# Latent attention's opening in another order, and the softmax sums spread over partitions by transposition and DMA instead of TensorE

## The chip, the cores and the metric

The kernel runs on one core of one Trainium2 chip. The metric is the device time of one execution in microseconds (us). Engines: TensorE (PE; its weight loads PEld), VectorE (DVE), ScalarE (ACT), GpSimd (POOL), and SyncE (SP), which here only issues DMAs.

## What is computed

Two layers of a streaming encoder on a sequence of 512 tokens, width 1024. A layer is half a SwiGLU, a mixer, half a SwiGLU, each behind an RMS norm. The first layer's mixer is pooling beside "forgetting" attention (8 heads); the second layer's is latent attention (MLA, 16 heads). The part that the change touches:

```python
def mla_mixer(h, cos, sin, w_in, q_norm, kv_norm, w_q_b, w_kv_b, w_out):
    proj = h @ w_in
    c_q  = proj[..., :256]; c_kv = proj[..., 256:384]
    k_rope = apply_rope(proj[..., 384:], cos, sin)
    q  = (rms_norm(c_q, q_norm) @ w_q_b).reshape(b, s, 16, 96)    # 64 plain + 32 rotary
    kv = (rms_norm(c_kv, kv_norm) @ w_kv_b).reshape(b, s, 16, 128) # 64 keys + 64 values
    ...
    y = blocked_attention(qk, k, v, 96 ** -0.5, CHUNK)   # softmax(q k^T + mask) v
    return y.reshape(b, s, 1024) @ w_out
```

## The kernel before

Activations lie transposed: 128 channels on the partitions, 512 tokens along the free axis. Every product is made in three passes: each operand is split into a rounded part and its rest (`hi` on ACT, `lo` on DVE, or on POOL where code says `nc.gpsimd`), and `mm3` (L178 to L180) adds rounded by rounded, rest by rounded and rounded by rest. Weights come through a ring of three raw tiles, whose loads (L189) SP issues in program order; a load waits until the split of an older tile has freed its buffer. A scheduler orders the instructions of every engine; `keep_in_program_order` holds the order of TensorE's products in the opening of MLA (`self.ordered`).

**The opening of MLA** (L1145 to L1320). `latent(n)` makes one of four projections of 24 products: 0 is the key/value latent, 1 and 2 the query latent, 3 the rotary keys. Each is multiplied by `rstdB`, the RMS factor of the incoming norm (`scaled`, L1145). `sums` (L364 to L386) sums squares by products with a column of ones (L371) and makes the factor `rt`, tokens on partitions; `spread` (L392) broadcasts `rt` over the partitions by products with the identity matrix, and ACT copies the result out of PSUM (L396). Three such factors are made: of the incoming norm, of the key/value latent (`rkv`) and of the query latent. `rotations` makes the tables `rota` and `rotb` from the last one (L1183, L1186), and a `query` is a product of 6 passes times such a table (L1248). The rotary keys are made last (L1173 to L1176).

**The heads.** Per head: scores on TensorE (mask added by L785), row minimum on DVE (L806), exponential on ACT with the row sums written into `sm` (L809), transposition of the probabilities on TensorE (L842), product with the values (`weighted`, L862, L866, L867). Two heads make a pair. After the pair's second `weighted`, `divided` takes the reciprocal of the eight columns of `sm` (L819), broadcasts it by eight products with the identity (L823, 16 records in the trace) into a bank of PSUM, and multiplies `y` by that bank (L827). `y` is then split into `yh` and `yl` for the output projection. `divided` runs for 4 pairs of the first mixer and 8 pairs of MLA. `keys_values` and `query` of the next pairs are made between the heads, and stand ready to fill TensorE while a softmax is under way.

Of the kernel before, what the change touches and what calls it, by code (L numbers as in the profile page):

```python
# [97 lines left out]
class Trunk:  # L98
    def __init__(self, ctx, tc, d, out):
        self.tc, self.nc, self.d, self.out = tc, tc.nc, d, out  # L100
        self.n = 0
        self.last = []
        self.pending = self.ordered = False
        self.then = None
        self.sums_of = []
# [257 lines left out]

    def sums(self, n, then=None):  # L364

# [11 lines left out]
        act = nc.scalar.activation  # L377
        act(root, ps[:, 0:blocks], AF.Sqrt, bias=self.eps[:, 1:2], scale=4.0 / n)
        act(ms, ps[:, 0:blocks], AF.Identity, bias=self.eps[:, 0:1], scale=1.0 / n)
        squared = act(rr, root, AF.Square, scale=0.5)  # L380
        if then is not None:
            self.table(then, squared)

# [4 lines left out]
        def spread(rstdB):  # L388

            pb = self.bank("pc")[:, 0 : blocks * P]  # L390
            for t in range(blocks):
# [3 lines left out]
                ))  # L395
            nc.scalar.activation(rstdB, pb, AF.Copy)  # L396
            self.rt = rt
# [392 lines left out]

    def probabilities(self, pool, sc, e):

# [14 lines left out]
        for i in (3, 2, 0, 1):  # L807
            bank, ps, cs = sc[i]
            self.exp = nc.scalar.activation(  # L809
                pr[bank][:, cs], ps[:, cs], AF.Exp, bias=mn[:, i : i + 1],  # L810
                scale=-1.0, accum_out=sm[:, i : i + 1],
            )
        return pr
# [127 lines left out]
    def pool_fox(self, next_col):  # L941
        nc, d = self.nc, self.d
        with self.tc.tile_pool(name=self.name("fox"), bufs=1) as pool:
# [63 lines left out]
            def head_scores(head, q1, q2, k1, k2):  # L1007
# [8 lines left out]

                return self.probabilities(pool, self.scores(block, self.causal), head % 2)

# [109 lines left out]
    def mla(self, next_col):  # L1128
        nc, d = self.nc, self.d
        wm = d["w_mla"]  # L1130
        with self.tc.tile_pool(name=self.name("mla"), bufs=1) as pool:
# [10 lines left out]

            def scaled(ps, first=None):
                t = self.temp()
                nc.vector.tensor_tensor(t, ps, self.rstdB, op=ALU.mult)  # L1145
                if first is not None:
                    self.square_into(t, first, not first)
                return t

            def parts(n, t, gcol):  # L1150
# [6 lines left out]
            rows_of = (slice(0, 64), slice(64, P))  # L1157

            self.ordered, self.pending = True, False
            rkv = ptile("rkv", dt=F32)  # L1160
            ps = latent(0)
            spread = self.sums(D)
            ps, ps1 = latent(1, 3, lambda: spread(self.rstdB)), ps
            ckv = scaled(ps1, True)
            spread_kv = self.sums(P)
            ps, ps1 = latent(2, 3, lambda: spread_kv(rkv)), ps
            cq = [parts(0, scaled(ps1, True), C_QN)]
            nc.vector.tensor_tensor(ckv, ckv, rkv, op=ALU.mult)
            ckvh, ckvl = parts(2, ckv, C_KVN)
            cq.append(parts(1, scaled(ps, False), C_QN + 1))  # L1170
            spread_q = []
            t = scaled(latent(3, 5, lambda: spread_q.append(self.sums(2 * P, AF.Exp))))
# [3 lines left out]
            nc.vector.tensor_tensor(t[0:64, :], t[0:64, :], s[0:64, :], op=ALU.add)  # L1176
            rot = [ptile("rota", dt=F32), ptile("rotb", dt=F32)]

            def rotations():
                rq = ptile("rkv", dt=F32)  # L1180
                spread_q[0](rq)
                for e in range(2):
                    nc.vector.tensor_scalar(  # L1183
                        rot[e][rows_of[e], :], rq[rows_of[e], :], -MLA_SCALE, None, op0=ALU.mult
                    )
# [3 lines left out]
                    )  # L1189


            keys = [[(self.xh[2 * e + m], self.xl[2 * e + m]) for m in range(2)] for e in range(2)]
            queries = [(self.xh[4 + m], self.xl[4 + m]) for m in range(4)]
            for e in range(2):
                for kh, _ in keys[e]:
                    self.hi(kh[rows_of[1 - e], :], t[0:64, :])
            for e in range(2):
                for _, kl in keys[e]:
                    self.lo(kl[rows_of[1 - e], :], t[0:64, :], keys[1][0][0][0:64, :])

            units = {}
            self.first = []

            def keys_values(pair):

                both = pair % 2 == 0
                cols = slice(0, 7 * P) if both else slice(7 * P, 12 * P)
                if True:
                    units[pair] = wh, wl = self.unit(
                        d["w_qkv"][pair // 2][:, cols], 5 + 2 * both, pool=pair > 0  # L1210
                    )
                m = pair % 2
                pk = self.bank("pa")
                self.mm3(pk, wh[:, 4, :], wl[:, 4, :], ckvh, ckvl, True, True)
# [14 lines left out]
                for half in range(2):  # L1229
                    pv = self.bank("pa")  # L1230
                    for t in range(2):
                        tok = slice((2 * half + t) * P, (2 * half + t + 1) * P)
                        self.mm3(pv[:, 2 * t * P : 2 * (t + 1) * P], ckvh[:, tok], ckvl[:, tok],
                                 vwh, vwl, True, True)
# [18 lines left out]
            def head_scores(head):  # L1253
# [9 lines left out]
                mask = self.chunked.rearrange("p a b -> p (a b)")  # L1263
                return self.probabilities(pool, self.scores(block, mask), head % 2)

# [15 lines left out]

            keys_values(0)
            query(0)
            query(1)
            self.ordered = False
            done = None
# [5 lines left out]
            for head in range(MLA_HEADS):  # L1292
                pr = head_scores(head)
                if head % 2 == 0 and head + 2 < MLA_HEADS:
                    keys_values(head // 2 + 1)
                if head + 2 < MLA_HEADS:
                    query(head + 2)
# [150 lines left out]
```

## Time and profile before

| | before |
|---|---|
| median of 3 runs | 1787.09 us (1785.72 to 1788.37) |
| the profiled execution | 1785.65 us |
| its span, first to last instruction | 1783.9 us |
| PE busy in the span | 1758.2 us (99%) |
| DVE, ACT, POOL busy | 1441.4, 925.2, 199.6 us |

The profile comes from one execution; its span is the time between its first and last instruction. A busy PE means that a matmul was under way. Idle time before an instruction is put down to what released it. The first mixer lies at about 395 to 525 us, MLA's opening at 1224 to 1270 us, MLA's heads up to about 1407 us.

### The profile page before, as it was taken

Reading aid. Unit: us, or ns where it says so; the run is one execution under the profiler, and the core shown is the slowest. Engines: PE = TensorE matmul, PEld = TensorE weight load, DVE = VectorE, ACT = ScalarE, POOL = GpSimd, SP = SyncE. Lnnn points to the kernel's source line nnn. Section 1 sums busy time; section 2 is a strip of 40 time slices with the busy share of each in tenths; the row PEclk is TensorE's granted clock in tenths of the full one; section 3 lists DMA queues with packets and bytes.
Section 4 is the critical chain, followed back from the end, with each engine's and each line's share of the span. In section 5 each row is a group of like instructions: output and inputs, shape, how many; then the busy total and the mean of one; then the engine's idle time right before and its main releaser. Section 6 shows DMA issues by size and latency. Waiting matters only on the chain.

```text
span 1783.9 us, 28548 instructions
## 1 busy us (share of the span) xinstructions
PE 1758.2 (99%) x11444; PEld 1586.0 (89%) x11444; DVE 1441.4 (81%) x2197; ACT 925.2 (52%) x1524; POOL 199.6 (11%) x156
## 2 busy tenths in 40 slices
PE   8999999999999999999999999999899999999998
PEld 6999999888888999999899999998788799999997
DVE  7988888657859988887699998975777799888874
ACT  7444444446647444444555444444777574444444
POOL 2000000113340000000200000002545200000002
PEclk9999999999999999999999999999999999999999
DMA  5333333313122333333233333341102123433331
GB/s 180 94 119 107 95 107 107 94 52 97 60 70 77 114 118 103 104 102 119 78 94 108 109 109 100 97 131 47 46 27 59 52 92 103 122 96 107 105 97 48
DMA packets 48933, 167.07 MB, mean 94 GB/s; under 512 B 5536, under 2 KB 7584, under 8 KB 48800
## 3 DMA queue, kind: packets, MB, share of 16 engines
q1 hardware_dynamic: 48800, 165.25, 30.3%
q8 instruction: 89, 1.46, 0.3%
q14 instruction: 44, 0.36, 0.1%
HBM read 163.14 MB, written 2.10 MB: 93 GB/s over the span
## 4 chain that ended last, share of the span: by engine, by line
PE 73%; DVE 2%; ACT 1%; issue 0%; POOL 0%; DVEq 0%; ACTq 0%; POOLq 0%
PE pa L178 10%; PE pa L180 10%; PE pa L179 10%; PE px L178 7%; PE px L180 7%; PE px L179 7%; PE pz L180 4%; PE pz L178 4%; PE pz L179 4%; PE py L180 2%; PE py L178 2%; PE py L179 2%; PE px L842 1%; PE pc L178 1%; PE pc L180 1%; PE pc L179 1%
## 5 line engine op out<-in xcount | busy, mean ns | idle before, releaser
L160 ACT ACTIVATE wh<-raw 128x1024 fp32r<-128x1024 f32 (+2 forms) x233 | 236.3, 1018 | 166.9 <-PE px L179 56.0
L165 DVE TENSOR_TENSOR wl<-raw,wh 128x1024 fp32r<-128x1024 f32 (+1 forms) x200 | 240.5, 1205 | 28.9 <-ACT wh L160 28.5
L347 POOL TENSOR_TENSOR acc<-acc,sq 128x512 f32<-128x512 f32 (+1 forms) x48 | 63.3, 1320 | 1066.1 <-ACT sq L341 1065.5
L618 DVE SCALAR_TENSOR_TENSOR h<-pa,h 128x512 f32<-128x512 f32 (+1 forms) x200 | 133.0, 666 | 58.9 <-PE pa L180 57.6
L180 PE MATMUL pa<-hh,wl 128*128 128x512 f32 (+1 forms) x432 | 165.9, 384 | 0.0
L179 PE MATMUL pa<-hl,wh 128*128 128x512 f32 (+1 forms) x432 | 165.6, 383 | 0.0
L178 PE MATMUL pa<-hh,wh 128*128 128x512 f32 (+1 forms) x432 | 165.2, 383 | 0.0
L180 PE MATMUL px<-xh,wl 128*128 128x256 f32 (+1 forms) x484 | 140.4, 291 | 0.5 <-DVE wl L165 0.5
L178 PE MATMUL px<-xh,wh 128*128 128x256 f32 (+1 forms) x484 | 139.7, 291 | 1.1 <-ACT wh L160 1.1
L179 PE MATMUL px<-xl,wh 128*128 128x256 f32 (+1 forms) x484 | 140.3, 290 | 0.0
L160 ACT ACTIVATE wh<-s 128x1024 fp32r<-128x1024 f32 (+1 forms) x51 | 51.2, 1008 | 153.0 <-PE px L179 134.3
L160 ACT ACTIVATE vh<-raw 128x1024 fp32r<-128x1024 f32 x83 | 87.7, 1059 | 72.9 <-PE px L179 38.7
L179 PE MATMUL pa<-hl,vh 128*128 128x512 f32 (+1 forms) x304 | 115.2, 380 | 0.0
L178 PE MATMUL pa<-hh,vh 128*128 128x512 f32 (+1 forms) x304 | 114.9, 381 | 0.0
L180 PE MATMUL pa<-hh,vl 128*128 128x512 f32 (+1 forms) x304 | 114.0, 380 | 0.0
L165 DVE TENSOR_TENSOR vl<-raw,vh 128x1024 fp32r<-128x1024 f32 x83 | 101.1, 1219 | 9.3 <-ACT vh L160 9.1
L178 PE MATMUL pz<-eh,wh 128*128 128x256 f32 x388 | 108.5, 280 | 0.0
L180 PE MATMUL pz<-eh,wl 128*128 128x256 f32 x388 | 108.4, 279 | 0.0
L179 PE MATMUL pz<-el,wh 128*128 128x256 f32 x388 | 108.4, 279 | 0.0
L178 PEld LDWEIGHTS px<-xh,wh 128*128 128x128 f32 x484 | 90.4, 188 | 5.8 <-ACT wh L160 1.5
L180 PEld LDWEIGHTS px<-xh,wl 128*128 128x128 f32 x484 | 90.8, 188 | 3.7 <-DVE wl L165 1.0
L179 PEld LDWEIGHTS pa<-hl,wh 128*128 128x128 f32 x432 | 81.2, 188 | 14.5
(410 smaller groups left out, 5599.0 us busy)
## 6 DMA issues: line engine op xcount, KB each, us to landing
raw<-in_w_gu_dram SPq DMA_DIRECT2D x172, 512.0 KB, 3.6
raw<-in_w_dn_dram SPq DMA_DIRECT2D x88, 512.0 KB, 3.7
raw<-in_w_ab_dram SPq DMA_DIRECT2D x24, 512.0 KB, 3.6
raw<-in_w_mla_dram SPq DMA_DIRECT2D x12, 512.0 KB, 3.5
h<-in_x_dram SPq DMA_DIRECT2D x8, 256.0 KB, 5.5
raw<-in_w_qkv_dram SPq DMA_DIRECT2D x4, 448.0 KB, 3.3
raw<-in_w_gu_dram SPq DMA_DIRECT2D x6, 256.0 KB, 5.5
out_dram<-h SPq DMA_DIRECT2D x4, 384.0 KB, 3.0
```

The costliest lines, as they stand in the source:

```text
L160: return self.nc.scalar.activation(out, in_, AF.Copy, scale=scale)
L165: return nc.vector.tensor_tensor(out, in_, hi.bitcast(F32), op=ALU.subtract)
L178: self.pe(mm(out, ah, bh, start=start, stop=False, **kw))
L179: mm(out, ah, bl, start=False, stop=False, **kw)
L180: mm(out, al, bh, start=False, stop=stop, **kw)
L347: (nc.vector if last else nc.gpsimd).tensor_tensor(acc, acc, sq, op=ALU.add)
L618: self.mark = nc.vector.scalar_tensor_tensor(h, ps, 0.5, h, op0=ALU.mult, op1=ALU.add)
L842: self.pe(nc.tensor.transpose(ps[:, c0 : c0 + P], pr[sb][:, s0 : s0 + P], self.ident))
```

## The change

The opening of MLA now makes the rotary keys' projection first, then the two query latents, then the key/value latent. The query and key/value latents are no longer multiplied by `rstdB`: their squares are summed raw, straight from PSUM, and the small number under the root is scaled instead (`above`). The query factor is spread in the middle of the key/value projection, and ACT and DVE read it from PSUM. Four queries (heads 0 to 3) are made before the first scores; the first keys are made from the raw latent and multiplied by `rkv` after the product, and the raw latent is multiplied by `rkv` for the values (L1290). The query sums take two groups of ones products where one stood.

In the heads, the eight sums of a pair, as soon as the second head's exponentials are done, are inverted into the first 8 columns of a 128x32 tile (`over`), turned by DVE's 32x32 transposition, written by four DMAs into a row in DRAM, and read back by two DMAs that give every one of 64 partitions the row of its head (into `acc`). `divided` multiplies `y` by `acc`. The last pair of each mixer keeps the TensorE products. So 3 pairs of the first mixer and 7 of MLA change.

```diff
@@ sums
+        else:
+            nc.vector.scalar_tensor_tensor(
+                ms, ps[:, 0:blocks], 1.0 / n, above, op0=ALU.mult, op1=ALU.add
+            )
+            act(root, ms, AF.Sqrt, scale=4.0)
+            nc.vector.scalar_tensor_tensor(
+                rr, root, 0.25, root, op0=ALU.mult, op1=ALU.mult
+            )
...
-            nc.scalar.activation(rstdB, pb, AF.Copy)
+            if rstdB is not None:
+                nc.scalar.activation(rstdB, pb, AF.Copy)
@@ probabilities
+        if e and last:
+            self.over.append(self.sums_of.pop(0))
+        elif e:
+            sm = self.sums_of.pop(0)
...
+            nc.vector.memset(over[:, 8:32], 0.0)
+            nc.vector.reciprocal(over[:, 0:8].rearrange("p (e t) -> p e t", e=2), sm)
+            nc.vector.transpose(turned, over)
+            row = self.dram.tile([2, S], F32, name=self.name("row"), tag="row", bufs=2)
+            for b in range(4):
+                nc.sync.dma_start(
+                    row.rearrange("e (t b c) -> b (e t) c", b=4, c=32)[b],
+                    turned[32 * b : 32 * b + 8, :],
+                )
+            for n, rows in enumerate(HALVES):
+                nc.sync.dma_start(self.acc[rows, :], row[n, :].partition_broadcast(64))
+            self.over.append(None)
@@ divided
-        sm = self.sums_of.pop(0)
+        sm = self.over.pop(0)
+        if sm is None:
+            nc.vector.tensor_tensor(y, y, self.acc, op=ALU.mult)
+            return
@@ mla, the opening
-            ps = latent(0)
+            ps_r = latent(3)
             spread = self.sums(D)
...
+            ps_kv = self.bank("pb")
+            for b in range(KC):
+                if b == 2:
+                    queries_sums()
+                if b == 6:
+                    rotations()
+                self.mm3(ps_kv, wkv[0][:, b, :], wkv[1][:, b, :], self.xh[b], self.xl[b],
+                         b == 0, b == KC - 1)
@@ keys_values
                 if pair == 0:
-                    rotations()
-                tk = self.temp()
-                nc.scalar.activation(tk, pk, AF.Copy)
+                    query(2)
+                    spread(rkv)
+                    with self.soon():
+                        nc.vector.tensor_tensor(tk, pk, rkv, op=ALU.mult)
+                    query(3)
+                    t = self.temp()
+                    nc.vector.tensor_tensor(t, ps_kv, rkv, op=ALU.mult)
+                    ckv = parts(2, t, C_KVN)
+                else:
+                    nc.scalar.activation(tk, pk, AF.Copy)
```

**The end of MLA's opening on TensorE.** `ch` and `cl` are the latents' parts, `xh_65`/`xl_73` the first head's keys before and `xh_67`/`xl_75` after, `px` the spread factor. Before:

```order
L178 MATMUL pa_12769<-ch_1896_12653,wh_12722 128x512
L179 MATMUL pa_12769<-cl_1897_12654,wh_12722 128x512
L180 MATMUL pa_12769<-ch_1896_12653,wl_12723 128x512
L178 MATMUL pa_12828<-ch_1892_12644,wh_12824 128x512
L179 MATMUL pa_12828<-cl_1893_12645,wh_12824 128x512
L180 MATMUL pa_12828<-ch_1892_12644,wl_12825 128x512
L178 MATMUL pz_12791<-xh_65,xh_69 128x512
L179 MATMUL pz_12791<-xl_73,xh_69 128x512
```

After:

```order
L406 MATMUL px_12776<-ident,rt_12747 128x128 x4
L181 MATMUL pa_12783<-ch_1888_12599,wh_12756 128x512
L182 MATMUL pa_12783<-cl_1889_12600,wh_12756 128x512
L183 MATMUL pa_12783<-ch_1888_12599,wl_12757 128x512
L181 MATMUL pa_12783<-ch_1895_12636,wh_12756 128x512
L182 MATMUL pa_12783<-cl_1896_12637,wh_12756 128x512
L183 MATMUL pa_12783<-ch_1895_12636,wl_12757 128x512
L181 MATMUL pz_12830<-xh_67,xh_71 128x512
L181 MATMUL py_12831<-xh_67,xh_71 128x384
L181 MATMUL pz_12832<-xh_67,xh_71 128x256
```

Before, the query of head 0 and the keys of the second pair stand ahead of the first scores; now the spread of the key/value factor and the query of head 3 do.

**The same place on VectorE.** `t` are products with the tables or with `rkv`, `mn` the row minima of head 0. Before:

```order
L1173 TENSOR_TENSOR t_12704<-t_12704,rope 128x512
L1175 COPY t_12707<-t_12704 64x512
L1176 TENSOR_TENSOR t_12704<-t_12704,t_12707 64x512
L1183 TENSOR_SCALAR rota_12710<-rkv_12730 64x512
L1186 SCALAR_TENSOR_TENSOR rota_12710<-rkv_12730,rope 64x512
L1183 TENSOR_SCALAR rotb_12711<-rkv_12730 64x512
L1186 SCALAR_TENSOR_TENSOR rotb_12711<-rkv_12730,rope 64x512
L165 TENSOR_TENSOR eh_81<-pc_12747,eh_81 128x2x128
L1248 TENSOR_TENSOR t_12776<-pa_12769,rota_12710 128x512
```

After:

```order
L400 TENSOR_TENSOR rt_12747<-root_12745,rr_12746 128x4
L1323 TENSOR_TENSOR t_12772<-pa_12765,rota_12640 128x512
L1287 TENSOR_TENSOR t_12764<-pc_12760,rkv_12505 128x512
L1323 TENSOR_TENSOR t_12790<-pa_12783,rotb_12641 128x512
L1290 TENSOR_TENSOR t_12794<-pz_12648,rkv_12505 128x512
L170 SCALAR_TENSOR_TENSOR cl_1936_12797<-t_12794,par,ch_1935_12796 128x512
L821 TENSOR_REDUCE mn_12848<-pz_12830 128x1
```

The rotary keys and the tables have moved well ahead; what now stands between the factor `rt` and the first row minimum is the key product (L1287), two queries and the values' latent (L1290, L170).

**The first pair of MLA on VectorE**, from its last `weighted` (`sq` is the pair's `y`) to the next pair's sums. Before:

```order
L867 TENSOR_TENSOR sq_12915<-pc_13032,sq_12915 64x512
L806 TENSOR_REDUCE mn_13177<-pz_13159 128x1
L827 TENSOR_TENSOR sq_12915<-sq_12915,pa_13044 128x512
L165 TENSOR_TENSOR tl_13071<-px_13065,th_13070 128x512
L819 RECIPROCAL sm_12971<-sm_12971 128x8
```

After:

```order
L904 TENSOR_TENSOR sq_12938<-pa_13055,sq_12938 64x512
L854 TENSOR_TENSOR sq_12938<-sq_12938,acc 128x512
L1323 TENSOR_TENSOR t_13143<-pc_13136,rotb_12641 128x512
L168 TENSOR_TENSOR tl_13084<-px_13078,th_13083 128x512
L836 RECIPROCAL over_13124<-sm_12994 128x8
```

The multiplication keeps its place, with `acc` in SBUF in place of the bank in PSUM; the first pair's own reciprocal and transposition (L836, L837) stand 20 rows ahead of it. Behind it wait a query's product and a split of transposed probabilities.

**SP's queue there.** Before:

```order
L189 DMA raw_13738<-in_w_mla_dram 128x1024
L189 DMA raw_13819<-in_w_qkv_dram 128x896
L189 DMA raw_14042<-in_w_qkv_dram 128x640
L189 DMA raw_14168<-in_w_mla_dram 128x1024
L189 DMA raw_14391<-in_w_mla_dram 128x1024
```

After:

```order
L192 DMA raw_13769<-in_w_mla_dram 128x1024
L192 DMA raw_13850<-in_w_qkv_dram 128x896
L840 DMA row_12931<-turned_12927 8x32 x4
L845 DMA acc<-row_12931 64x512 x2
L192 DMA raw_14075<-in_w_qkv_dram 128x640
L840 DMA row_13129<-turned_13125 8x32 x4
L845 DMA acc<-row_13129 64x512 x2
L192 DMA raw_14203<-in_w_mla_dram 128x1024
```

The six DMAs of a pair stand between two weight loads, and a load behind them is issued after them.

## Rows read from the trace of the kernel before

**Rows 1.** The page's part 1: busy time, share, instructions.

```profile
PE 1758.2 (99%) x11444; PEld 1586.0 (89%) x11444; DVE 1441.4 (81%) x2197; ACT 925.2 (52%) x1524; POOL 199.6 (11%) x156
```

**Rows 2.** Windows: first mixer, MLA's first head, MLA's heads; length, then busy us per engine.

```profile
395.00:525.00 130.00, 129.32 (x719) 107.44 (x718) 89.28 (x151) 73.73 (x154) 53.43 (x38) 1.00 0.26 78
...
1255.00:1285.00 30.00, 24.34 (x135) 19.75 (x135) 23.65 (x44) 22.58 (x55) 17.70 (x12) 0.94 0.15 45
1285.00:1400.00 115.00, 114.74 (x759) 96.46 (x757) 84.42 (x162) 86.29 (x215) 49.23 (x31) 1.00 0.14 40
```

**Rows 3.** Waits of PE over the span: us, times, longest.

```profile
PE pa L178 <- DVE t L1248: 4.6, 1, 4.6
...
PE pz L180 <- POOL xl L1251: 0.9, 1, 0.9
PE px L392 <- DVE rt L386: 0.8, 1, 0.8
```

**Rows 4.** Chain that ended last, MLA's opening: start, us, what.

```profile
1253.27 1.97 DVE t L1173
...
1257.84 1.66 DVE rota L1186
...
1261.52 0.79 PE pa L178
```

**Rows 5.** Windows: the stretch behind PE's longest wait; the last three are clock, DMA share, GB/s.

```profile
1261.50:1264.95 3.45, 3.43 (x10) 2.95 (x10) 3.44 (x4) 0.63 (x1) 1.65 (x1) 0.51 0.02 5
```

**Rows 6.** Groups by line and form: the division's products.

```profile
L823 PE MATMUL pa<-ident,sm 128*64 128x128 f32 x160 | 12.4, 282 | 0.0
...
L823 PE MATMUL pc<-ident,sm 128*64 128x128 f32 x32 | 2.2, 279 | 0.0
```

**Rows 7.** Timeline of PE around one division: start, us, instruction.

```profile
1356.41 0.40 PE L179 MATMUL pz<-xl,xh 128*128 128x512 f32 x1
1356.74 1.09 PE L823 MATMUL pa<-ident,sm 128*64 128x128 f32 x16
1357.76 0.50 PE L178 MATMUL pc<-ch,wh 128*128 128x512 f32 x1
1358.10 0.39 PE L179 MATMUL pc<-cl,wh 128*128 128x512 f32 x1
1358.33 0.40 PE L180 MATMUL pc<-ch,wl 128*128 128x512 f32 x1
```

**Rows 8.** Chain that ended last: one group of ones products.

```profile
1229.95 0.79 PE px L371 x8
```

**Rows 9.** Timelines of ACT, DVE and POOL in MLA's opening.

```profile
1254.14 0.60 ACT L396 ACTIVATE rkv<-px 128x512 f32<-128x512 f32 x1 [1.08 <-PE px L392]
...
1272.30 1.28 ACT L160 ACTIVATE xh<-t 64x512 fp32r<-64x512 f32 x2
...
1269.12 0.69 DVE L1248 TENSOR_TENSOR t<-pa,rota 128x512 f32<-128x512 f32 x1 [0.65 <-PE pa L180]
...
1249.08 0.74 DVE L167 SCALAR_TENSOR_TENSOR cl<-t,par,ch 128x512 fp32r<-128x512 f32 x1
...
1276.57 2.65 POOL L1223 TENSOR_TENSOR xl<-t,xh 64x512 fp32r<-64x512 f32 x2
```

**Rows 10.** Timeline of DVE: reciprocal and multiplication of MLA's seventh pair.

```profile
1381.51 0.18 DVE L819 RECIPROCAL sm<-sm 128x8 f32<-128x8 f32 x1
...
1393.29 0.68 DVE L827 TENSOR_TENSOR sq<-sq,pa 128x512 f32<-128x512 f32 x1
```

**Rows 11.** The queue SP, one issue; and DMA issues: count, KB each, us to landing.

```profile
1272.10 0.33 SPq L189 DMA_DIRECT2D raw<-in_w_mla_dram  x1
...
raw<-in_w_mla_dram SPq DMA_DIRECT2D x12, 512.0 KB, 3.5
...
out_dram<-h SPq DMA_DIRECT2D x2, 256.0 KB, 2.9
...
par<-in_par_dram SPq DMA_DIRECT2D x1, 48.5 KB, 1.8
```

More of the change, by code (lines that the diff above doesn't have):

```diff
@@ L104, in __init__ @@
         self.then = None
-        self.sums_of = []
+        self.sums_of, self.over = [], []
+        self.dram = ctx.enter_context(
+            tc.tile_pool(name="dram", bufs=2, space=bass.MemoryType.DRAM)
+        )
         self.state = ctx.enter_context(tc.tile_pool(name="state", bufs=1))
@@ L362, in table, with sums @@
             self.nc.scalar.activation(self.warm, self.warm, func)
-    def sums(self, n, then=None):
+    def sums(self, n, then=None, above=None):
         nc = self.nc
@@ L377, in sums @@
         act = nc.scalar.activation
[L378 to L382, printed above, removed]
+        if above is None:
+            act(root, ps[:, 0:blocks], AF.Sqrt, bias=self.eps[:, 1:2], scale=4.0 / n)
+            act(ms, ps[:, 0:blocks], AF.Identity, bias=self.eps[:, 0:1], scale=1.0 / n)
+            squared = act(rr, root, AF.Square, scale=0.5)
+            if then is not None:
+                self.table(then, squared)
+        else:
[6 more added lines that the diff above has]
+            )
+        self.ms = ms
         nc.vector.tensor_tensor(rr, rr, ms, op=ALU.add)
@@ L789, in scores, with probabilities @@
         return out
-    def probabilities(self, pool, sc, e):
+    def probabilities(self, pool, sc, e, last):
         nc = self.nc
@@ L1015, in block @@
                                      skip_group_check=True)
-                return self.probabilities(pool, self.scores(block, self.causal), head % 2)
+                return self.probabilities(pool, self.scores(block, self.causal), head % 2,
+                                          head > FOX_HEADS - 3)
             def head_values(head, pt):
@@ L1159, in mla, with squares @@
             self.ordered, self.pending = True, False
+            def squares(ps):
+                sq = self.ring("sq", 2)
+                nc.scalar.activation(sq, ps, AF.Square)
+                return sq
             rkv = ptile("rkv", dt=F32)
-            ps = latent(0)
+            ps_r = latent(3)
             spread = self.sums(D)
[L1163 to L1172, printed above, removed]
+            above = ptile("above", dt=F32, shape=(P, TB))
+            nc.vector.tensor_scalar(above, self.ms, EPS, None, op0=ALU.mult)
+            ps = latent(1, 3, lambda: spread(self.rstdB))
+            t = self.temp()
+            with self.soon():
+                nc.vector.tensor_tensor(t, ps_r, self.rstdB, op=ALU.mult)
             nc.vector.tensor_tensor(t, t, self.rope, op=ALU.mult)
@@ L1192, in mla, with rotary @@
+            with self.soon():
+                ckv = parts(2, ps_kv, C_KVN)
+                sq = [squares(ps_kv)]
             keys = [[(self.xh[2 * e + m], self.xl[2 * e + m]) for m in range(2)] for e in range(2)]
             queries = [(self.xh[4 + m], self.xl[4 + m]) for m in range(4)]
[L1194 to L1199, printed above, removed]
+            def rotary(m):
+                for e in range(2):
+                    self.hi(keys[e][m][0][rows_of[1 - e], :], t[0:64, :])
+                for e in range(2):
+                    self.lo(keys[e][m][1][rows_of[1 - e], :], t[0:64, :],
+                            keys[1][m][0][0:64, :])
@@ L1201, in mla, with qkv_unit @@
+            rotary(0)
             units = {}
             self.first = []
-            def keys_values(pair):
+            def qkv_unit(pair):
                 both = pair % 2 == 0
                 cols = slice(0, 7 * P) if both else slice(7 * P, 12 * P)
[L1208 to L1211, printed above, removed]
+                units[pair] = self.unit(
+                    d["w_qkv"][pair // 2][:, cols], 5 + 2 * both, pool=pair > 0
+                )
@@ L1263, in head_scores @@
                 mask = self.chunked.rearrange("p a b -> p (a b)")
-                return self.probabilities(pool, self.scores(block, mask), head % 2)
+                return self.probabilities(pool, self.scores(block, mask), head % 2,
+                                          head > MLA_HEADS - 3)
             def head_values(head, pt):
@@ L1280, in head_values @@
                     self.lo(yl[pair], self.y, yh[pair])
-            keys_values(0)
+            qkv_unit(0)
             query(0)
             query(1)
+            self.squares = sq
+            with self.soon():
+                spread = self.sums(P, None, above)
+            qkv_unit(1)
+            keys_values(0)
+            rotary(1)
             self.ordered = False
@@ L1295, in mla @@
                     keys_values(head // 2 + 1)
-                if head + 2 < MLA_HEADS:
+                if 3 < head + 2 < MLA_HEADS:
                     query(head + 2)
```

40 lines of the change are left out of this document (28 added, 12 removed).

## The prediction, made before the changed kernel ran

> **What bounds the kernel now.** I read the page's busy shares first: PE works 1758.2 of 1783.9 us, so only TensorE work that goes, or TensorE's few gaps, can move the time [rows 1]. The windows by stage say where: in the first mixer and in MLA's heads PE is busy all but 0.7 and 0.3 us of the stretch, while DVE has 0.7 of it and ACT 0.57 and 0.75. Only around MLA's first head does PE stand, 24.3 of 30 us busy [rows 2]. PE's waits name the gaps there: 4.6 us for the first query's product on DVE, 0.9 for a POOL split, 0.8 for a norm factor [rows 3]; the FFNs are not touched. The chain of waits tells why the long one is there: the rotary keys come from the last projection, and behind it DVE makes them, both tables and the product in one line, some at 1.97 and 1.66 us apiece, from 1253.3 to 1261.5 [rows 4]. After that wait PE's granted clock is 0.51 for 3.45 us, the lower of its two levels (1.2 GHz); it had stood idle just before [rows 5]. What ran in that stretch would have needed half, so 1.7 us are lost. In all the opening loses 4.6 + 0.9 + 0.8 + 1.7 = 8.0 us.
>
> **The division's products.** A pair's eight products are 16 records on PE; 160 + 32 records are 12 pairs, of which 10 now go [rows 6]. Their price is not the 1.09 us of the row but the distance between neighbours: from the product ahead to the one behind 1.35 us, of which 0.23 is the spacing of two such products: 1.12. The product behind takes 0.34 to its successor in place of 0.23, so up to 1.23 in all; where a transposition stands behind, the extra 0.11 need not be there [rows 7]. I take 1.15, near the lower end since both kinds of neighbour occur: 10 x 1.15 = **11.5 us** (11.2 to 12.3).
>
> **What takes their place.** The reciprocal remains. A memset, a transposition of 128x32 and a multiplication come on DVE; the multiplication takes the place of one of 0.68 us [rows 10]. With both operands in SBUF it lies between that and the 1.97 us of the rope product, which also has both there [rows 4]; ten of them are at most 13 us of DVE, off the path while DVE is busy 0.73 of MLA's heads. I take nothing for them. If that cover goes, they cost up to 1.3 us each.
>
> **The DMAs.** For the first time DVE waits for a transfer inside a softmax. Four issues of 0.33 us, the landing of the last write, two issues, the landing of the second read. The smallest transfer shown lands in 1.8 us; of those that write DRAM the quicker kind takes 2.9, for 256 KB. So 1.3 + 1.8 + 0.7 + 1.8 = 5.6 to 1.3 + 2.9 + 0.7 + 2.9 = 7.8 us, and up to 11.3 if a weight load of 3.5 us is in front [rows 11]. I take 7, near the middle, as a write of 1 KB is smaller than either row's. What is there to hide it: from reciprocal to multiplication 11.8 us in MLA's seventh pair, the shortest distance of the ten [rows 10]; the new order keeps about as many instructions between. TensorE's saving takes about 1 us of it, which leaves 10.6. So 7 fits and 11.3 just does not. Cost taken: 0, bounds 0 and 0.7 a pair. What is queued behind the waiting multiplication is the next query's product and a split of probabilities, for which PE waits; what is queued behind the DMAs on SP are weight loads that are issued long before their use.
>
> The Trainium skill, "DMA: Bandwidth & Descriptors", section "Rules for kernel authors", speaks against this part: many small transfers should be joined into a large one, since under 64 KB a transfer is mostly overhead. Its section "Anatomy of one DMA — SWDGE (gpsimd) path" states about 2.0 us fixed for each, so six in a row would be an estimated 12 us, against 4 + 2.0 of issues = 6.0 if those of a kind overlap; the row's 1.8 us for 48.5 KB agrees with its size, and nothing in this trace shows six in a row.
>
> **The opening.** What goes: the 8.0 us. What is late next I follow from the spread of `rkv` on, in the order shown. PE has one query behind it, six products of 0.23 and 0.11 for the change of kind, 1.5 us [rows 7]. The first scores need: ACT's split of a query that stands ahead (0.64), the copy of `rkv` (0.60), DVE's key product (0.69), ACT's split of the keys (0.64), with hand-overs 2.9 us. **Gap 1.4.** Three score passes of 0.55 us in all then need the rest of the keys from POOL, 1.3 for 64x512: **gap 0.75**. The values' latent uses a buffer that POOL frees only after a second such split: 1.3 + 0.69 (multiplication) + 0.64 (split on ACT) = 2.65, against 1.6 of remaining scores: **gap 1.05**; its rest on DVE takes 0.74, against two short products: **gap 0.5** [rows 9]. That is 3.7 us, in pieces a third of the old wait; I take no fall of the clock. Further, two queries' products (12 x 0.23 = 2.8 us) stood behind the first scores and covered head 0's softmax; now they stand ahead, and the way from those scores through DVE and ACT to the first transposed probabilities is as long as it was. Price 0 to 2.8; I take 2, since DVE and ACT, on that way, are busy 23.7 and 22.6 of 30 us there [rows 2]. The query sums gain one group of ones products, 0.8 us [rows 8]. Sum: 8.0 - 3.7 - 2.0 - 0.8 = **1.5 us** (from 7.2 with no new wait to -0.8 with waits as long as the old).
>
> **What may not come back.** In MLA's heads PE waits for nothing, with ACT busy 0.75 of it. With 8 of 115 us of TensorE work gone, ACT is at 0.81: still not the bound as a mean, but a head whose exponentials come late will show as a new wait. I take 1 us lost (0 to all 7 x 1.15 = 8).
>
> **Sum.** 11.5 + 1.5 - 1.0 = 12.0 us. The profiled execution has a span of 1783.9 and a time of 1785.65; 12 less is a span of 1771.9 and a time of 1773.65. The median of the three runs lies 1.44 above the profiled time, so I forecast **1775.1 us**.
>
> **The rivals.**
> 1. The opening gets no new waits: 7.2 in place of 1.5, and nothing lost in the heads: 1787.1 - 12.3 - 7.2 = 1767.6. For it speaks that the longest wait's line on DVE is taken apart; against it the walk above.
> 2. MLA's heads turn to ACT as their bound: 8 of the 11.5 us do not come back, 3.5 + 1.5 = 5.0, so 1782.1. For it: from 1255 to 1285 ACT is busy 0.75 while PE still has gaps. Against: over the heads the same 0.75 leaves 29 us of ACT idle [rows 2].
> 3. **Slower.** The six transfers of a pair land one after another: 4 x 2.9 + 2 x 2.6 (between the 1.8 and 2.9 of rows 11, nearer the upper, as they read what was just written) = 16.8 us, 5 more than the 11.8 in which they must be done, plus 1 for the shorter time: 6 us of DVE standing in each of MLA's seven pairs. Less what TensorE has in hand, one query of 1.4 us, it is 4.6 x 7 = 32, and 1775 + 32 = 1807. It decides from the point at which the seven stalls eat the 12 us: a chain of about 10.6 + 1.4 + 1.7 = 13.7 us. Against it: the four writes are issued without a wait between them.
> 4. In between: single pairs land late, behind a load that stands in front on SP's queue, 1 to 1.7 us in half of the pairs: about 1780 to 1787.
>
> **How the numbers follow.** Forecast with its own bounds, 1771 to 1779: 0.60. Rival 1, 1767 to 1771: 0.11. Rival 2, 1779 to 1783.5: 0.14. Rival 4: 0.08, half of it under 1783.5. Slower: 0.07. A measurement of this kernel tells 0.2% (3.6 us) from no change: faster is under 1783.5, slower over 1790.7. Faster: 0.60 + 0.11 + 0.14 + 0.04 = 0.89; same 0.04; slower 0.07. The range that leaves out no more than 2 in 10 is 1767.5 to 1782.5: it has the forecast, rival 1, and most of rival 2.
>
> **What would show it.** PE has 32 records of the division's products in place of 192, and its busy time falls by some 10 us. The 4.6 us wait on DVE is gone, and with it the stretch at half clock; in its place stand waits of 0.5 to 1.5 us, for ACT's key split, POOL's rest of the keys and ACT's and DVE's parts of the values' latent. DVE's `y` by `acc` waits for no DMA, or for under 1 us; the row writes land in 2 to 3 us. I am wrong if DVE stands at `acc` in most pairs and PE behind it (rivals 3, 4), if PE waits for ACT's exponentials in many heads (rival 2), or if a gap of over 3 us remains in the opening, with a fall of the clock.

## The result, and the profile after

The changed kernel takes 1774.28 us, the median of four executions (1772.60 to 1776.14), beside 1786.86 us for the kernel before in its four (1785.72 to 1788.37). The ratio is 0.9929 (95%: 0.9912 to 0.9947): 12.6 us less, of which the interval leaves 9.5 to 15.7. The forecast was 1775.1. The profiled execution took 1774.27 us, its span is 1772.6.

The page's busy times of the kernel after, the line that answers to [rows 1]:

```profile
PE 1747.6 (99%) x11292; PEld 1578.4 (89%) x11292; DVE 1440.0 (81%) x2218; ACT 925.5 (52%) x1520; POOL 200.2 (11%) x156
```

PE's work is 10.6 us less, and DVE's is no longer than before (1440.0 us for 1441.4): what left TensorE was the bound, what came to DVE was not. The line of the division's products after, with duration in ns (least, median, most), first and last start:

```profile
L860 PE MATMUL pc<-ident,sm x16: 272/273/323, 516.0 to 516.9; 128*64 128x128 f32 x16
L860 PE MATMUL pa<-ident,sm x16: 272/273/323, 1393.2 to 1394.0; 128*64 128x128 f32 x16
```

Two pairs are left, one at the end of each mixer, in place of the twelve of [rows 6]. The windows of after for the stretches of [rows 2] (length, then busy us of PE, PEld, DVE, ACT, POOL, then clock, DMA share, GB/s):

```profile
395.00:525.00 130.00, 127.21 (x668) 106.18 (x667) 89.00 (x153) 72.26 (x153) 54.83 (x38) 0.97 0.29 84
...
1255.00:1285.00 30.00, 26.62 (x162) 21.07 (x163) 20.84 (x46) 24.29 (x60) 18.96 (x13) 1.00 0.19 53
1285.00:1400.00 115.00, 113.45 (x683) 96.45 (x682) 88.85 (x175) 87.80 (x214) 49.73 (x31) 1.00 0.20 59
```

MLA's first head has 3.4 us of PE's idle time left of 5.7, and its clock is whole again (1.00 for 0.94). The heads behind it have 1.6 for 0.3; 0.4 of that is a wait behind the last weighted product, where the kernel before has one of 1.4 outside its window. What was not foreseen stands in the first line: in the first mixer PE now has 2.8 us of idle time for 0.7, and a granted clock of 0.97. The waits of PE over the span (us, times, longest) name it; they answer to [rows 3]:

```profile
PE pc L181 <- DVE t L1129: 2.7, 1, 2.7
...
PE py L181 <- ACT pr L824: 1.2, 2, 0.6
PE pa L181 <- ACT t L1293: 1.1, 2, 0.6
...
PE px L406 <- DVE rt L400: 0.9, 1, 0.9
PE pz L181 <- ACT xh L163: 0.8, 1, 0.8
```

The 4.6 us wait of MLA's opening is gone. Four short ones stand there. The longest wait of these is new and lies in the first mixer: a projection waits until DVE has made `t`, the input of a pooling window, from the PSUM bank that the projection needs next. Behind it TensorE runs at the lower of its two levels (1.2 GHz), as it did behind the old wait [rows 5]:

```profile
450.10:455.80 5.70, 5.67 (x15) 4.41 (x15) 1.86 (x6) 0.78 (x2) 2.34 (x4) 0.50 0.44 133
```

5.67 us of work at a clock of 0.50 is work for half that time, so 2.8 us are lost there on top of the 2.7. How long the clock stays low is not the same in every execution. In e6 below, behind the same wait of 2.7 us:

```profile
452.30:455.70 3.40, 3.40 (x11) 2.62 (x10) 0.46 (x2) 0.28 (x2) 1.10 (x2) 0.51 0.54 152
```

That is 3.4 us at half clock, so 1.7 lost, and the traces of e2, e7 and e8 have some 3.3 to 3.4 us as well. What makes it longer here, no run shows.

Why `t` comes late is read from DVE's and POOL's timelines of after, around that wait (start, us, engine, line, instruction):

```profile
446.75 2.73 DVE L168 TENSOR_TENSOR yl<-sq,yh 128x512 fp32r<-128x512 f32 x1
449.40 0.68 DVE L1129 TENSOR_TENSOR t<-pc,rstdB 128x512 f32<-128x512 f32 x1
...
446.12 2.81 POOL L210 TENSOR_TENSOR wl<-raw,wh 128x1024 fp32r<-128x1024 f32 x1 [6.33 <-ACT wh L163]
```

And from the same place of the kernel before:

```profile
446.74 0.69 DVE L165 TENSOR_TENSOR yl<-sq,yh 128x512 fp32r<-128x512 f32 x1
447.35 0.20 DVE L819 RECIPROCAL sm<-sm 128x8 f32<-128x8 f32 x1
447.46 0.64 DVE L1091 TENSOR_TENSOR t<-pa,rstdB 128x512 f32<-128x512 f32 x1
...
448.27 1.04 POOL L1095 TENSOR_TENSOR t<-t 128x511 f32<-128x511 f32 x1 [8.56 <-DVE t L1091]
449.25 0.19 POOL L1096 COPY t<-t 128x1 f32<-128x1 f32 x1
449.39 2.40 POOL L207 TENSOR_TENSOR wl<-raw,wh 128x1024 fp32r<-128x1024 f32 x1
```

DVE reaches the split of `y` within 0.01 us of its old time. It takes 2.73 us in place of 0.69, and ends 0.55 us behind POOL's split of a weight, which started before it (446.12 to 448.93). In the kernel before, that split of a weight stood behind the pooling sum on POOL's queue and came 3.3 us later, beside DVE work that reads PSUM.

The opening after, in PE's timeline, the instructions that waited:

```profile
1258.71 1.13 PE L406 MATMUL px<-ident,rt 128*128 128x128 f32 x8 [0.85 <-DVE rt L400]
...
1261.99 0.50 PE L181 MATMUL pz<-xh,xh 128*128 128x512 f32 x1 [0.75 <-ACT xh L163]
...
1263.34 0.50 PE L182 MATMUL pz<-xl,xh 128*128 128x512 f32 x1 [0.28 <-POOL xl L1298]
...
1270.91 0.50 PE L181 MATMUL pa<-ch,wh 128*128 128x512 f32 x1 [0.48 <-ACT t L1293]
```

The first scores start at 1262.0, the first exponential runs at 1265.8 (1266.9 before), though two queries' products now stand ahead of it.

The transfers of MLA's seventh pair, from DVE's and SP's timelines; they answer to [rows 10, 11]:

```profile
1371.64 0.19 DVE L836 RECIPROCAL over<-sm 128x8 f32<-128x8 f32 x1
1372.70 0.20 DVE L837 STREAM_TRANSPOSE turned<-over 128x32 f32<-128x32 f32 x1
...
1382.57 0.68 DVE L854 TENSOR_TENSOR sq<-sq,acc 128x512 f32<-128x512 f32 x1
...
1372.93 1.30 SPq L840 DMA_DIRECT2D row<-turned  x4
1375.25 1.09 SPq L845 DMA_DIRECT2D acc<-row  x2
```

The reads are issued 2.3 us behind the first write; the multiplication stands 10.9 us behind the reciprocal, and in the other six pairs 11.4 to 14.7. DVE waits for `acc` nowhere in this trace.

### The profile page after: what moved, and what is told of

It is laid out like the page before. It is cut to its first block, busy times and chain, and to the rows that moved or that the text cites. A ratio compares the mean times of both kernels' runs of the same rounds, so it can differ in the third digit from the quotient of the medians.

```text
span 1772.6 us, 28369 instructions
## 1 busy us (share of the span) xinstructions
PE 1747.6 (99%) x11292; PEld 1578.4 (89%) x11292; DVE 1440.0 (81%) x2218; ACT 925.5 (52%) x1520; POOL 200.2 (11%) x156
## 4 chain that ended last, share of the span: by engine, by line
PE 95%; DVE 2%; ACT 2%; issue 1%; DMA 0%; POOL 0%; SPq 0%; DVEq 0%; ACTq 0%; POOLq 0%
PE pa L181 12%; PE pa L183 12%; PE pa L182 12%; PE px L183 9%; PE px L181 9%; PE px L182 9%; PE pz L182 5%; PE pz L183 5%; PE pz L181 5%; PE py L183 2%; PE py L181 2%; PE py L182 2%; PE pc L181 2%; PE pc L182 2%; PE pc L183 2%; PE pa L899 1%
```

## The experiments

All times are medians; "the changed kernel" is the one above, 1774.3 us, and the kernel before ran beside each group at 1786.8 to 1787.2. Stage times are differences of starts in PE's timeline: the first mixer from its first mask product to its last weighted product (108.93 us before, 109.78 after), MLA from the first product of its opening to its last weighted product (180.92 and 167.71).

**e1: the opening alone.**

```diff
-        if e and last:
+        if e:
```

> The new opening with every pair's division back on TensorE. Theory A (the prediction's walk: 8.0 us of old waits, 3.7 + 2.0 of new ones and 0.8 of added products): 1.5 us under the kernel before, some 1785.5. Theory B (read from the two traces: from the first product of the opening to the last weighted product the changed kernel is 13.2 us shorter, of which seven pairs' divisions are 8.05): some 5 us under the kernel before, 1782.

1782.75 us, ratio 0.9976 (0.9968 to 0.9985): 4.3 us less, with 2.7 to 5.7 in the interval. Theory B. The prediction's 1.5 for the opening was too little. MLA takes 176.37 us here and 167.71 in the changed kernel, so seven pairs' divisions are worth 8.66, 1.24 each: in MLA's heads all of it comes back. The two stages do not end at quite the same work: the last pair's division products stand ahead of the last weighted product in e1 (1399.9) and behind it in the changed kernel (1393.2). Counted from the opening to the end of the program the difference is 8.5, 1.21 each.

**e2: the division alone.** The code of `probabilities` and `divided` from the change, put into the kernel before, with its old opening.

> The old opening with ten divisions moved to DVE and the DMAs. Theory A (each division worth 1.15 us wherever it stands, 1 us not coming back): 10.5 us under the kernel before, 1776.5. Theory B (the three of the first mixer bring 3.45 us but open a wait of 2.7 us and a stretch at half clock that costs 2.9, so that stretch ends later than before): 11.5 - 5.6 = 5.9 us under it, some 1781.

1780.20 us, 0.9959 (0.9945 to 0.9973): 6.9 us less (4.8 to 9.8). Theory A's 10.5 is outside, B's 5.9 inside. PE's wait of 2.7 us for `t` is there, beside the opening's old 4.6.

**e3: the first mixer's pairs back on TensorE.**

```diff
-                                          head > FOX_HEADS - 3)
+                                          True)
```

> The changed kernel with the first mixer's four divisions on TensorE, those of MLA's heads as in the changed kernel. Theory A (1.15 us a pair): 3.45 us over the changed kernel, 1777.7. Theory B (the wait and the half clock of the first mixer go with them): 5.6 - 3.45 = 2.1 us under the changed kernel, 1772.2, and PE's wait of 2.7 us for DVE's t is not in the trace.

1774.55 us, 0.9931 (0.9919 to 0.9944): the changed kernel's time, between the two theories. The wait for `t` is gone as B says, but not the 2.1 us in the time. By the stage, the first mixer takes 108.91, 0.87 less than in the changed kernel; but e2, e6, e7 and e8, with the three divisions by DMA and the same wait, take 108.37 to 108.61 there. So the three divisions bring about as much as they lose, and the mechanism of B stands with a balance near nothing. The profiled execution also lost time ahead of the mixer: in it the granted clock is 0.53 from 35.5 to 38.9 us, where the changed kernel's is whole.

**e4: the rotation of PSUM buffers.** With the division's products a step in the rotation `pa`, `pa`, `pc` had gone as well, and two projections in a row had come to use the single `pc`.

```diff
         if sm is None:
+            next(self.tags["pa"])
             nc.vector.tensor_tensor(y, y, self.acc, op=ALU.mult)
```

> The changed kernel, but a division by DMA takes a step in the rotation of PSUM buffers (two of pa, one of pc), as the division on TensorE did. Theory B1 (the 2.7 us wait is there because, with that step gone, two projections in a row use the single pc buffer): the wait and the half clock are gone, 5.6 us under the changed kernel, 1768.7. Theory B2 (it is there because a POOL split now runs beside a DVE split, which takes 2.73 us in place of 0.69): PE still waits about 2 us there, and the time is within 1 us of the changed kernel's 1774.3.

1777.54 us, 0.9942 (0.9929 to 0.9954). The wait is as long as it was, now in the other buffer (PE's waits in the first mixer):

```profile
PE pa L181 <- DVE t L1130: 2.7, 1, 2.7
PE px L880 <- DVE tl L168: 1.8, 1, 1.8
PE pz L1052 <- DVE k L168: 0.4, 1, 0.4
```

The timelines of DVE and POOL there:

```profile
448.28 2.73 DVE L168 TENSOR_TENSOR yl<-sq,yh 128x512 fp32r<-128x512 f32 x1
...
447.65 2.81 POOL L210 TENSOR_TENSOR wl<-raw,wh 128x1024 fp32r<-128x1024 f32 x1 [6.33 <-ACT wh L163]
```

The split of `y` still takes 2.73 us beside POOL's. Theory B1 falls: another buffer helps nothing while `t` is late. B2's wait is there, but not its time, which is 3.3 us over the changed kernel where it allowed 1: the order that this edit gave has a second wait of 1.8 us, and this profile too has a fall of the clock at 35 us.

**e5 and e11: that one split on DVE.** One of the first mixer's weights is split by DVE, behind `t`; DVE's order ahead of it is unchanged.

```diff
-                return self.project(*self.unit(wab[n], pool=n > 5))
+                return self.project(*self.unit(wab[n], pool=n > 5 and n != 14))
```

> The changed kernel with one weight split of the first mixer (the one that POOL does at 446.1 us of the changed trace, beside DVE's split of y) moved from POOL to DVE, behind DVE's t; DVE's order ahead of that is word for word the same. Theory B2 (the POOL split holds DVE's split of y at 2.73 us in place of 0.69, so t comes 2.0 us late): y's split takes 0.7, PE's wait of 2.7 us falls to under 1, the half clock behind it is gone, and the time is about 5 us under the changed kernel, 1769. Theory B3 (the wait comes from the transfers of the sums, as rival 4 of the prediction had it): the wait stays at over 2 us, and the time at 1774.

> The kernel of e5 once more, beside that of e10 on one chip. Both theories: 1769.4, 5 us under the changed kernel.

1769.41 and 1769.44 us, 0.9902 (0.9889 to 0.9916) and 0.9900 (0.9886 to 0.9915): 4.9 us under the changed kernel, with executions from 1769.2 to 1770.4 that don't touch its 1772.6 to 1776.1. DVE's timeline in e5, then PE's waits in the first mixer (all of them), then the window of the old half clock:

```profile
446.68 0.69 DVE L168 TENSOR_TENSOR yl<-sq,yh 128x512 fp32r<-128x512 f32 x1
447.29 0.68 DVE L1129 TENSOR_TENSOR t<-pc,rstdB 128x512 f32<-128x512 f32 x1
447.89 1.22 DVE L168 TENSOR_TENSOR wl<-raw,wh 128x1024 fp32r<-128x1024 f32 x1
```

```profile
PE pc L181 <- DVE t L1129: 0.7, 1, 0.7
```

```profile
450.10:455.80 5.70, 5.70 (x34) 4.67 (x32) 4.46 (x13) 4.07 (x12) 1.20 (x3) 1.00 0.42 127
```

The same split of `y` takes 0.69 without POOL beside it, `t` starts 2.1 us earlier, the wait is 0.7, and the clock stays whole. Theory B2, with its number. The first mixer takes 105.11 us: 3.82 less than before the change, so its three divisions are worth what MLA's are. It is 4.67 less than in the changed kernel and 3.3 to 3.5 less than in e2, e6, e7 and e8, where the half clock is shorter: that is what the collision cost.

**e6 and e7: a longer way for the sums.** Two or four more transfers of 4 KB in a row, DRAM to DRAM.

```diff
+            for _ in range(2):
+                row, was = self.dram.tile([2, S], F32, name=self.name("row"), tag="hop", bufs=8), row
+                nc.sync.dma_start(row, was)
             for n, rows in enumerate(HALVES):
                 nc.sync.dma_start(self.acc[rows, :], row[n, :].partition_broadcast(64))
```

> The changed kernel with two more transfers in a row (4 KB, DRAM to DRAM) between the row writes and the reads into acc; the order on DVE is unchanged. In the changed trace the way from reciprocal to landed acc takes 5.6 to 8.1 us, and the multiplication stands 10.9 to 14.7 us behind the reciprocal in MLA's heads. At an estimated 2.3 us a transfer the way is 11 us. Theory C1 (there is slack, as the prediction had it): within 1 us of the changed kernel. Theory C2 (the landing already sets when the multiplication runs): 4.6 us later in each of MLA's seven pairs, up to 20 us slower.

> The same with four more transfers: at 2.3 us each the way is 15.6 us, over all seven distances of MLA's heads (11.4, 13.1, 13.8, 12.2, 14.7, 13.4, 10.9), by 4.2, 2.5, 1.8, 3.4, 0.9, 2.2 and 4.7, sum 19.7. Theory C1 with one query of 1.4 us as TensorE's reserve: DVE stands at acc in most pairs, and 19.7 - 7 x 1.4 = some 10 us are lost, 1784. If nothing waits behind the multiplication that PE needs soon: under 3 us, 1777. If all that DVE loses is lost: 1794.

e6: 1773.79 us, 0.9924 (0.9911 to 0.9938), as the changed kernel. SP's timeline of one pair:

```profile
1276.70 1.30 SPq L840 DMA_DIRECT2D row<-turned  x4
1278.95 2.38 SPq L846 DMA_DIRECT2D row<-row  x2
1282.73 1.11 SPq L848 DMA_DIRECT2D acc<-row  x2
```

From the first added transfer to the reads are 3.8 us, 1.9 for each, and nothing is lost: DVE waits for `acc` nowhere. e7: 1783.54 us, 0.9981 (0.9972 to 0.9990), 9.3 over the changed kernel where 10 were expected. DVE's waits, then the timelines of DVE and SP for one of them:

```profile
DVE sq L857 <- DMA acc<-row: 15.5, 7, 3.0
```

```profile
1293.23 0.19 DVE L836 RECIPROCAL over<-sm 128x8 f32<-128x8 f32 x1
1307.57 0.69 DVE L857 TENSOR_TENSOR sq<-sq,acc 128x512 f32<-128x512 f32 x1 [2.20 <-DMA acc<-row]
...
1296.75 5.98 SPq L846 DMA_DIRECT2D row<-row  x4
1304.08 1.10 SPq L848 DMA_DIRECT2D acc<-row  x2
```

Here the way decides: 1307.57 - 1293.23 = 14.3 us from reciprocal to landing, of which 1304.08 - 1296.75 = 7.3 are the four added. So the changed kernel's own way is 7.0 us, of which the reads are the last 3.5 (1304.08 to 1307.57). e6's was then 10.8, just under the shortest cover of 10.9. That 9.3 came so near to 10 is in part luck: the 10 were 19.7 us of stalls less 1.4 in hand for each pair, and measured are 15.5 us of stalls, of which (15.5 - 9.3) / 7 = 0.9 a pair did not reach the time.

**e8: the third and fourth query behind the scores again.**

```diff
-                    query(2)
...
-                    query(3)
...
-                if 3 < head + 2 < MLA_HEADS:
+                if head + 2 < MLA_HEADS:
```

> The changed kernel with the third and fourth query product of the opening put back behind the first scores, where the kernel before had them. Theory D1 (the prediction's step: as cover of head 0's softmax they are worth 2.0 us, ahead of the scores 2.8): under 1 us slower than the changed kernel, 1775. Theory D2 (behind the scores nothing was uncovered without them): the full 2.8 us of new waits ahead of the first scores, with half clock behind them 1.4 to 1.7 more, 1777 to 1779.

1776.24 us, 0.9943 (0.9929 to 0.9957): 2.0 over the changed kernel, but the intervals overlap, so the time alone doesn't decide. PE's timeline in the opening does for its first half:

```profile
1257.81 1.13 PE L406 MATMUL px<-ident,rt 128*128 128x128 f32 x8 [2.22 <-DVE rt L400]
...
1261.02 0.80 PE L181 MATMUL pz<-xh,xh 128*128 128x512 f32 x1 [2.08 <-ACT xh L163]
```

The two waits ahead of the first scores grow from 0.85 and 0.75 to 2.22 and 2.08, and the clock falls to 0.50 behind them. From the opening's start to the first exponential e8 needs 0.43 us more with 2.8 us less to do. From there to the last weighted product it needs 0.97 more with 2.8 us more to do: 1.8 of the 2.8 cost nothing there. 1.4 of them is PE's idle time behind the first exponential (2.64 us in the changed kernel, 1.27 in e8). The division at that point is rough, since in e8 PE has also done some fewer products of the scores by then. Both theories were half right: as cover behind the scores the queries are worth 1.8, ahead of them more.

**e9: the second query's rest on DVE**, on top of e5.

```diff
-                nc.gpsimd.tensor_tensor(ql, tq, qh.bitcast(F32), op=ALU.subtract)
+                (nc.vector if head == 1 else nc.gpsimd).tensor_tensor(
+                    ql, tq, qh.bitcast(F32), op=ALU.subtract
+                )
```

> The kernel of e5 (a weight split moved to DVE), and in the opening the second query's rest is split by DVE in place of POOL. In the trace of the changed kernel DVE's 128x4 product of the norm factor takes 1.26 us and ends when POOL's split of that query ends, where the others of its size take 0.16; PE then waits 0.85 us for the factor. Theory F1 (a DVE instruction with both operands in SBUF is held while POOL runs): that product takes 0.16, PE's wait of 0.85 us falls to 0 to 0.3, and about 1 us is gained over e5's 1769.4, little more than the interval. Theory F2 (it is late for another reason, and DVE's 0.69 more comes on top): the wait grows to 1.5 us, 1770.

1770.43 us, 0.9909 (0.9894 to 0.9924): no gain over e5. First DVE's and POOL's timelines in the opening of the changed kernel, then DVE's and PE's in e9's:

```profile
1256.70 1.26 DVE L393 SCALAR_TENSOR_TENSOR rr<-root 128x4 f32<-128x4 f32 x1 [0.73 <-ACT root L392]
1258.00 0.16 DVE L398 TENSOR_TENSOR rr<-rr,ms 128x4 f32<-128x4 f32 x1
...
1255.27 2.68 POOL L1326 TENSOR_TENSOR xl<-t,xh 128x512 fp32r<-128x512 f32 x2 [1.04 <-ACT xh L163]
```

```profile
1253.08 0.16 DVE L393 SCALAR_TENSOR_TENSOR rr<-root 128x4 f32<-128x4 f32 x1
1253.27 0.16 DVE L398 TENSOR_TENSOR rr<-rr,ms 128x4 f32<-128x4 f32 x1
1253.77 0.69 DVE L1323 TENSOR_TENSOR t<-pa,rota 128x512 f32<-128x512 f32 x1 [0.33 <-PE pa L183]
1254.37 0.17 DVE L399 RECIPROCAL rr<-rr 128x4 f32<-128x4 f32 x1
...
1254.88 1.13 PE L406 MATMUL px<-ident,rt 128*128 128x128 f32 x8 [1.15 <-DVE rt L400]
```

F1's mechanism holds: without POOL the product of 128x4 takes 0.16 us in place of 1.26. Its gain doesn't come: the scheduler now puts the third query's product between `rr` and its reciprocal, where DVE waits 0.33 us for PE and works 0.69, and PE's wait grows from 0.85 to 1.15.

**e10 and e12: no division on TensorE at all**, on top of e5.

```diff
-        if e and last:
+        if False:
```

> The kernel of e5 with the last pair of each mixer divided by DMA as well, so no division on TensorE. In e5's trace MLA's last reciprocal is at 1379.6 us and its division's products at 1389.0, so the way of 5.6 to 8.1 us would fit into 9.5. Theory G1: two more pairs at 1.15 us each are gained, 1767. Theory G2 (behind the last weighted product PE waits for DVE's sum anyway, 0.38 us behind the division's 1.09, so those products fill a wait): no change, 1769.4. Theory G3 (the landing is late at the end, where nothing is left to cover it): slower, by up to 5 us with half clock.

> The kernel of e10 once more, beside that of e5. In the traces of the two the last pairs gain 1.0 us each between the last weighted product and the stage behind it, while e10's profile lost 1.7 at the start to a stretch at half clock which e5's had not. Theory G1 (that stretch belongs to single executions): 2.0 us under e11. Theory G2 (the last pairs bring nothing to the time): within 0.5 us of e11.

1769.05 and 1769.13 us, 0.9901 (0.9885 to 0.9918) and 0.9899 (0.9882 to 0.9915), 0.3 under e5 both times: no difference that can be told. G3 is out, the landing isn't late at the end. Between G1 and G2 it stays open: e12's profiled execution is 1.7 us under e11's, but the mean granted clock of the four executions is 0.997, 0.997, 0.996, 0.996 for 0.998, 0.998, 0.997, 0.997 in e11, and 0.001 of the span is 1.8 us. Why the clock is lower without these products wasn't tried.

## Why the prediction came out, point by point

The time came out 0.8 us from the forecast. Three of its terms came out too small by 1.0, 2.8 and 1.0 us, and a loss of 3.3 to 4.7 us was not in it; that these cancel so nearly is luck.

| term | forecast | measured | from |
|---|---|---|---|
| ten divisions | 11.5 | 12.5 | 8.66 for seven (e1), 3.82 for three (e5) |
| opening | 1.5 | 4.3 | e1 |
| transfers | 0 | 0 | e6 |
| not back in MLA's heads | -1.0 | 0 | e1 against the changed kernel |
| first mixer | 0 | -3.3 to -4.7 | e5 against e2, e6, e7, e8 and the changed kernel |
| sum | 12.0 | 12.1 to 13.5 | the whole change: 12.6 |

**The division's products: right, size a little low.** 1.24 (or 1.21, counted to the end of the program) and 1.27 us a pair, about the upper bound of 1.23; PE's busy time fell by 10.6 us, as forecast.

**The transfers: right.** The way was put at 7 us, e7 gives 7.0; the shortest cover at 10.6, the trace has 10.9. The parts were off in both directions: a read's issue is 0.55 us and not 0.33, the reads land 3.5 us behind their first issue, but the writes are done about a microsecond behind the last issue, earlier than the 1.8 of the nearest row, so that the reads are issued 2.3 us behind the first write. In e6 a transfer that waits for the one before it takes 1.9 us. The Trainium skill, "DMA: Bandwidth & Descriptors", section "Anatomy of one DMA — SWDGE (gpsimd) path", gives about 2.0 us of fixed cost; that is for transfers issued from GpSimd, and these are issued from SP, so the trace comes near the figure without testing it. Of the prediction's two estimates from it, the 6.0 us for writes and reads that overlap among themselves is near the 7.0 measured, the 12 us for six in a row is not. The warning of many small transfers in its "Rules for kernel authors" did not show in the time, since the way is off the path. Rival 3 is refuted as a forecast and confirmed as a mechanism: with a way of 14.3 us seven stalls, 15.5 us of DVE, cost 9.3, so the gain would be eaten somewhat beyond the 13.7 us that it named.

**The opening: the walk of new waits put them too high, and was not the whole of the miss.** It put 3.7 us at four places; the waits measured are 3.0. The key split on ACT cost 0.75 for 1.4, the rest of the keys on POOL 0.28 for 0.75, and the values' latent nothing for 1.05 + 0.5: DVE made `t` for it at 1262.0, right behind the last query, without a wait for a buffer of POOL's. The walk lacked one wait of 0.85 (`rt`) and two of 0.5 to 0.6 for ACT's key copy of the next pairs. The price of the two queries missing behind the scores, 2.0, was near: e8 has 1.8. All this is 0.7 and 0.2 us, a third of the 2.8 that the term was short. Another 1.0 to 1.4 lies where the forecast had nothing, at the end of MLA's heads: behind the last weighted product PE waits 1.4 us for DVE's sum of the last head in the kernel before and in e2, 0.4 in the changed kernel and in e8, and not at all in e1. Why the new opening changes the order there, no run shows, and the rest, 0.5 to 0.9, is within e1's interval. The old clock fall is gone, as forecast.

**MLA's heads: too cautious.** PE's idle time there, up to the last weighted product, rose from 0.3 to 1.2 us, for ACT's exponentials as rival 2 said, but the divisions' gain arrived in full. e1, with the divisions on TensorE, has 1.6 us there (118.19 us with PE busy 116.63), so the rise is no price of the divisions that left. Rival 2 is refuted: ACT is busy 87.8 of 115 us.

**The first mixer: the step that failed outright.** I read from [rows 2] that PE waits 0.7 us there with DVE busy 0.7 of it, priced the seven stalls of MLA, and took the three pairs here as free. The change moved no work onto the path; it moved `y`'s multiplication behind two splits and the row minima in DVE's order, and POOL's split of a weight ahead of a pooling sum. The split then met a DVE instruction that it had not met before. e5 shows the collision as the cause, e4 excludes the single buffer, e3 shows that it comes with the change's divisions. It cost 3.3 to 4.7 us where the term was 0. That the new place of the multiplication is why the scheduler put POOL's split earlier is read from the orders, and no run shows it.

I had the evidence in hand: [rows 4] has DVE products of 1.97 and 1.66 us that take 0.69 elsewhere, and POOL splits run beside both (from 1253.13 and from 1256.07). I used them as a bound for the duration of the new multiplication and did not ask what held them, so I did not look for what else POOL's queue could hold. The rule is in the Trainium skill, "SBUF — State Buffer", section "Who interferes with whom": a VectorE instruction with two inputs in SBUF and a GpSimd instruction that reads SBUF exclude each other for the whole instruction, and which of them was issued first decides who blocks. The trace agrees: 2.73 us for 0.69 beside POOL (e5 against the changed kernel), 1.26 for 0.16 (e9), and the multiplication by `acc` takes 2.15 us in one pair of ten and 0.68 to 0.95 in the others, while DVE's products that read PSUM keep their 0.68 beside a POOL split. e5 shows the other order too: there DVE's split of the weight starts first, at 447.89, and POOL's pooling sum, 1.04 us in the changed kernel, starts at 448.14 and takes 1.86.

## What to carry over

A sum of terms can be right while its terms are not: take the parts apart on the chip (each part alone, and each part undone) before trusting the account. When an edit changes durations, a scheduler moves other engines' work too, so compare the orders of the engines that share something with the one that waits (here POOL's splits beside DVE's products from SBUF), in every stage that the edit touches and not only where the gain lies. A chain of small DMAs is free as long as its length, here 7 us, stays under the distance to its use, and that distance can be measured by adding transfers until it shows.

## What was not expected of the hardware

- One POOL split beside a DVE split from SBUF cost 3.3 to 4.7 us: 2.04 us more on DVE made PE's wait 2.7 in place of 0.7, and the clock of 0.50 behind it took another 1.7 to 2.8, as it lasted 3.4 us in one execution (e6) and 5.7 in another.
- Four writes of 1 KB to DRAM are done about 1.0 us behind the last issue (1374.23 to 1375.25), while the reads that give 64 partitions the same row land 3.5 us behind the first issue.
- The granted clock falls for some 3.4 us at 35 us, behind a wait of 1.5 to 1.8 us for a split weight at 34 us, in some profiles (e3, e4, e7, e10) and not in the others, of which e8 has a wait of 1.8 as well. It is worth 1.7 us and blurs differences of that size.
